# Hybrid decoder trunk on one core: where two weight loads and three small steps stand around the first and the last group's turn through memory in the MLP

## The chip, the core and the metric

The kernel runs on one core of a Trainium2 chip. The metric is the device time of one execution in microseconds; below it is given as the median of three runs. The profile is of one more execution, taken by the hardware profiler; all times inside it count from its first instruction. The engines are named as in the profile: PE (matrix multiplies; PEld its weight loads), ACT (scalar engine), DVE (vector engine), POOL (general engine) and SP, whose queue issues nearly all transfers.

## What is computed

Two layers of a mixer and an MLP over 256 tokens of width 1024, in fp32. The change lies in the MLP:

```python
def squared_relu_mlp(h, w_up, w_down):
    return jnp.square(jax.nn.relu(h @ w_up)) @ w_down
...
        h = rms_norm(x, mlp_norm[l])
        x = x + squared_relu_mlp(h, w_mlp_up[l], w_mlp_down[l])
```

`w_up` is 1024x4096, `w_down` 4096x1024. Fp32 products are made of three matmuls of rounded parts: with a high part and a low part (the rest) of each operand, high x high, high x low, low x high (`three`, L301 to L304).

## The kernel before

**Weights.** All weights lie in one array in the order of use, in blocks of 512 KB. SP's queue transfers a block to one of seven `raw` buffers (L218); ACT copies it to `whi` (rounded high part, L281), DVE subtracts to get `wlo` (L283), which frees the raw buffer. There are six `whi` and six `wlo`; a buffer of these is freed when PE has used it. So SP issues a transfer when DVE has split the block seven places earlier in the order.

**The MLP.** The 4096 hidden columns go in eight groups of 512. For each group four blocks `up` (i = 4g to 4g+3) are multiplied into two PSUM banks `pup`, one for each half of the tokens. `squared_relu(g)` (L1334) then reads the two banks with ReLU on ACT (L1338), squares the two halves on ACT (L1340), and DVE transposes 32x32 blocks of each (L332, `hblocks`). SP writes the result to memory (L346, `bounce`) and reads it back in four pieces (L350, `hturned`), which completes the transpose. `h_ready` (L1354) splits that into high part (ACT, L323 `sq`) and low part (DVE, L323 `sq`), the operands of the four blocks `down` of this group. Ten ups are done ahead; then PE's order, written out by hand in `mlp_order`, is for each group 0 to 4: down 4g, two ups, downs 4g+2 and 4g+3 together, down 4g+1, two ups. Groups 0, 1, 2, 3, 4 and 6 do those two downs together with seven products instead of eight (`seven`, L1383). For this `fetch_sums` (L243) makes sums of the two blocks on DVE (L240: `wsum` of down 4g+2 alone; `tsums`, the inner sums, of both) and `h_sums` sums of the operand (L1377 to L1379). Two of the seven products go to the PSUM banks of the group g+2 of `pup`, which was read just before; DVE copies (first group) or adds these to `carried` (L1411), and after that the banks serve the ups of group g+3. So after group 0's seven products, up 12 writes its first half into the bank of the second product and its second half into that of the first one, each after DVE's copy of it.

**What sets the order.** PE's order is fixed by hand in this stretch. On SP, ACT and DVE a scheduler with a model of time sets the order when the program is built; each engine then runs its list strictly in that order. `tc.issue_after(x)` (used through the table `behind` in `have`, L203) makes what a block of code issues on the engine of `x` stand behind `x` in that engine's list. It adds no wait. `behind[key]` so pins the transfer (if x is a transfer), the high part (if x is on ACT) or the sums and low part (if x is on DVE) of the block `key`. Before, for the first group two such pins stand at L1344: the raw transfer of down 4 behind the group's last `hturned`, and down 2's work on DVE behind the group's last transpose. `order` holds the blocks not fetched yet.

Of the kernel before, what the change touches and what calls it, by code (L numbers as in the profile page):

```python
# [10 lines left out]
AF = mybir.ActivationFunctionType  # L11
# [10 lines left out]
NF = DFF // P  # L22
# [134 lines left out]
def trunk(ctx: ExitStack, tc: tile.TileContext, gx, wts, consts, gfin, gn, xtok, out):  # L157


    nc = tc.nc  # L160
# [31 lines left out]
    order, loaded = list(where), {}  # L192
# [8 lines left out]
    behind = {}  # L201

    def have(n):  # L203

        while len(loaded) < n:
            first = order.pop(0)
            with ExitStack() as pinned:
                for ins in behind.get(first, ()):
                    pinned.enter_context(tc.issue_after(ins.ins))
                loaded[first] = fetch(first)  # L210
# [81 lines left out]
    def misc_tile(name="misc"):  # L292
        return ps.tile([P, 512], F32, name=name, tag="misc", bufs=4)

    def w2k(name):
        return sb.tile([P, 512], F32, name=name, tag="w2k", bufs=W2K)
# [31 lines left out]
    def blocks_tile(name):  # L328
        return sb.tile([P, 4 * S], F32, name=name + "blocks", tag="probT", bufs=2)

    def turn_row(blocks, t, row):
        return nc.vector.transpose(blocks.rearrange("p (b j t e) -> p t j b e", b=4, j=4, t=2)[:, t], row)  # L332

    def turned_blocks(rows, name, tag, bufs, last=None, then=()):

        blocks = blocks_tile(name)
        for t in range(NT):
            turn = turn_row(blocks, t, rows[t])
        for key in then:
            behind.setdefault(key, []).append(turn)  # L340
        return turned_by_hbm(blocks, name, tag, bufs, last)

    def turned_by_hbm(blocks, name, tag, bufs, last=None):

        bounce = dr.tile([P, 4 * S], F32, name="bounce", bufs=2)
        nc.sync.dma_start(bounce, blocks)  # L346
        turned = sb.tile([P, 4 * S], F32, name=name + "turned", tag=tag, bufs=bufs)
        for b in range(4):
            src = bounce.rearrange("(a p) (b r) -> b p a r", a=4, b=4)[b]
            dma = nc.sync.dma_start(turned[32 * b : 32 * b + 32, :].rearrange("p (a r) -> p a r", a=4), src)  # L350
        if last:
            behind.setdefault(last, []).append(dma)
        return turned
# [458 lines left out]
    def layer(l, xn, before):  # L812
# [4 lines left out]
        b0 = []  # L817
# [490 lines left out]
        us, h2, latest = {}, {}, []  # L1308

        def up(i):  # L1310

            g, j = divmod(i, 4)
            if j == 0:
                us[g] = [misc_tile("pup") for _ in range(NT)]
            wh, wl = load_w(l, "up", g, j)
            for kk in range(2):
                k = 2 * j + kk
                ah, al = xm.k(k)
                for t in range(NT):
                    sl = slice(P * t, P * t + P)  # L1320
                    three(us[g][t], ah[:, sl], al[:, sl], wh[:, kk, :], wl[:, kk, :], k == 0, k == KD - 1)
            if i == 1:
                xm.stats(accs[3])
            if j == 3:
                if g - 2 in SEVEN[l]:
                    have(2)
                    if g == 2:
                        with tc.issue_after(latest[1].ins):
                            sums[0] = h_sums(waiting.pop(0))
                elif g == NF // 4 - 1 and g - 1 in SEVEN[l]:  # L1330
                    have(4)
                squared_relu(g)

        def squared_relu(g):  # L1334

            rows = [w2k("relu") for _ in range(NT)]
            for t in range(NT):
                relu = nc.scalar.activation(rows[t], us[g][t], AF.Relu, scale=xm.col[t])  # L1338
            for t in range(NT):
                nc.scalar.activation(rows[t], rows[t], AF.Square)  # L1340
            if g:
                waiting[g] = turned_blocks(rows, "h", "t4", T4)
            else:
                waiting[g] = turned_blocks(rows, "h", "t4", T4, (l, "down", 4, 0), [(l, "down", 2, 0)])  # L1344
            if SEVEN[l][0] <= g - 2 < NF // 4 - 3:
                behind.setdefault(order[3 if g - 2 in SEVEN[l] else 4], []).append(relu)
            if 1 < g < NF // 4 - 1:
                h_ready(g - 1, relu)
            elif g != 1:
                h_ready(g)  # L1350

        waiting = {}

        def h_ready(g, after=None):  # L1354

            turned = waiting.pop(g)
            sq = sb.tile([P, 2, 4, S], F32R, name="sq", tag=("Q", "KK")[g % 2], bufs=1)
            with ExitStack() as pinned:
                if after:
                    pinned.enter_context(tc.issue_after(after.ins))  # L1360
                latest[:] = split_turned(turned, [sq[:, i] for i in range(2)])
            for j in range(4):
                h2[4 * g + j] = sq[:, 0, j, :], sq[:, 1, j, :]
            if g in SEVEN[l]:
                if not g or g - 1 in SEVEN[l]:
                    waiting[g] = turned
                else:
                    sums[g] = h_sums(turned)
# [89 lines left out]
        last = l == L - 1  # L1458
# [61 lines left out]
        if not last:  # L1520
            xn = Normed(G_ATT + KD * (l + 1), KD - 2)
            ys = {}


            have(ENDS[l])
            for j in range(ENDS[l], 4):
                behind[l + 1, "b0", j] = latest
            have(4)

            def copied(q):  # L1530
                ys[q] = w2k("ydn")
                copy = nc.vector.tensor_add(ys[q], accs[q], share[q])
                if q == 0:
                    tc.keep_in_program_order(copy)

            def turned(q):
                t, half = quarters[q]
                pt = misc_tile("pyd")
                for i in range(4):
                    nc.tensor.transpose(pt[:, P * i : P * i + P], ys[q][:, P * i : P * i + P], ident)  # L1540
                x_t = X[half][:, :, P * t : P * t + P]
                add = nc.vector.tensor_add(x_t, x_t, pt.rearrange("p (k s) -> p k s", k=4))
                if q == 0:
                    tc.keep_in_program_order(add)
                return xn.take_part(t, half)

            for q in range(4):
                ends[q]()
                copied(q)
                if q:  # L1550
                    turned(q - 1)

            def before(i):
                if i == 2:
                    behind[l + 1, "mq", 0, 0] = turned(3)
                if i == 7:
                    order_pe.close()

            return xn, before
# [44 lines left out]
    for l in range(L):  # L1604
        xn, before = layer(l, xn, before)
# [14 lines left out]
T4 = 8  # L1620
# [82 lines left out]
```

## Time and profile before

| what | value |
|---|---|
| median of three runs | 808.08 us (807.4 to 808.43) |
| profiled execution | 807.2 us, span of its instructions 805.4 us, granted clock 0.998 |
| PE busy | 797.0 us, 99% of the span |
| DVE, ACT busy | 675.8 us (84%), 483.1 us (60%) |
| transfers of raw weights | 264 of 512 KB, 4.9 us median from issue to landing |
| bounce, hturned of the MLP and the mixer | 16 of 512 KB, 3.6 us; 64 of 128 KB, 3.2 us |

A row of a timeline gives the start, the duration (from the first start to the last end where several equal instructions are merged), engine, line and operation; in brackets stands how long the engine had been idle before it and what ended that. Matmuls overlap: each is shown as 0.39 us, but one starts about 0.23 us after the other when nothing holds them up, so a hold-up is read from the starts. The first layer's MLP lies at about 221 to 397 us, the second's at about 620 to 800 us.

### The profile page before, as it was taken

How to read it: one execution, taken by the hardware profiler on the slowest of the kernel's cores; microseconds unless marked ns; L12 is line 12 of the kernel's file. 1: busy time of each engine (PE TensorE's matmuls, PEld its weight loads, DVE VectorE, ACT ScalarE, POOL GpSimd, SP SyncE). 2: the span in 40 equal slices, each digit the busy share in tenths (PEclk: the TensorE clock that was granted, in tenths of full speed). 3: DMA queues.
4: the chain of work that ended last, by engine and by line, in shares of the span. 5: the costliest groups of instructions: out<-in, count | busy, mean ns of one | idle time of the engine just before them, and what ended most of it. 6: DMA issues, size and time to landing. Idle time of an engine off the chain costs nothing.

```text
span 805.4 us, 11403 instructions
## 1 busy us (share of the span) xinstructions
PE 797.0 (99%) x3915; PEld 665.1 (83%) x3915; DVE 675.8 (84%) x1136; ACT 483.1 (60%) x747; POOL 73.2 (9%) x63
## 2 busy tenths in 40 slices
PE   9999999999999999999999999999999999999996
PEld 7888887888888888888788888888888878888885
DVE  6769997978888898887797987699698878899786
ACT  7775654653557666666486566655545666667562
POOL 0100810000030000000025220000000300000000
PEclk9999999999999999999999999999999999999999
DMA  9975889975678677778656579688665687788741
GB/s 335 338 244 179 281 241 297 282 235 173 222 225 244 228 255 248 252 269 259 209 163 228 157 232 326 213 261 273 217 223 192 186 272 260 241 280 319 261 169 54
DMA packets 68122, 192.11 MB, mean 239 GB/s; under 512 B 8288, under 2 KB 25056, under 8 KB 67808
## 3 DMA queue, kind: packets, MB, share of 16 engines
q1 hardware_dynamic: 67488, 190.71, 72.4%
q8 instruction: 31, 0.51, 0.3%
q10 hardware_dynamic: 576, 0.67, 0.2%
q14 instruction: 27, 0.22, 0.1%
HBM read 168.81 MB, written 18.87 MB: 233 GB/s over the span
## 4 chain that ended last, share of the span: by engine, by line
PE 89%; DMA 5%; DVE 3%; ACT 1%; SPq 1%; issue 1%; DVEq 0%; ACTq 0%
PE acc L302 16%; PE acc L304 16%; PE acc L303 16%; PE pup L302 6%; PE pup L304 6%; PE pup L303 6%; PE acc L1273 6%; PE acc L515 4%; PE acc L517 2%; DMA raw<-wts 2%; DMA hturned<-bounce 2%; DMA bounce<-hblocks 1%; PE ps_s L1039 1%; PE acc L881 1%; DMA qkoth<-qkraw 1%; DVE wlo L283 1%
## 5 line engine op out<-in xcount | busy, mean ns | idle before, releaser
L281 ACT ACTIVATE whi<-raw 128x1024 fp32r<-128x1024 f32 (+3 forms) x263 | 264.8, 1019 | 170.5 <-PE acc L304 98.1
L283 DVE TENSOR_TENSOR wlo<-raw,whi 128x1024 fp32r<-128x1024 f32 (+3 forms) x263 | 313.8, 1209 | 48.9 <-ACT whi L281 46.1
L302 PE MATMUL acc<-whi,xs 128*128 128x512 f32 (+1 forms) x304 | 119.4, 394 | 0.2
L303 PE MATMUL acc<-wlo,xs 128*128 128x512 f32 (+1 forms) x304 | 117.8, 388 | 0.0
L304 PE MATMUL acc<-whi,xs 128*128 128x512 f32 (+1 forms) x304 | 117.7, 388 | 0.0
L303 PE MATMUL pup<-wlo,xs 128*128 128x512 f32 x256 | 99.8, 390 | 0.0
L304 PE MATMUL pup<-whi,xs 128*128 128x512 f32 x256 | 99.6, 389 | 0.0
L302 PE MATMUL pup<-whi,xs 128*128 128x512 f32 x256 | 99.4, 389 | 0.0
L304 PE MATMUL acc<-whi,sq 128*128 128x512 f32 x184 | 72.0, 391 | 0.7 <-DVE sq L323 0.5
L302 PE MATMUL acc<-whi,sq 128*128 128x512 f32 x184 | 71.8, 390 | 0.0
L303 PE MATMUL acc<-wlo,sq 128*128 128x512 f32 x184 | 71.6, 389 | 0.0
L302 PEld LDWEIGHTS acc<-whi,xs 128*128 128x128 f32 x304 | 57.0, 188 | 13.6 <-issue 0.8
L304 PEld LDWEIGHTS acc<-whi,xs 128*128 128x128 f32 x304 | 57.1, 188 | 11.3
L303 PEld LDWEIGHTS acc<-wlo,xs 128*128 128x128 f32 x304 | 57.1, 188 | 10.7
L304 PEld LDWEIGHTS pup<-whi,xs 128*128 128x128 f32 x256 | 48.1, 188 | 9.9
L303 PEld LDWEIGHTS pup<-wlo,xs 128*128 128x128 f32 x256 | 48.1, 188 | 9.8
L302 PEld LDWEIGHTS pup<-whi,xs 128*128 128x128 f32 x256 | 47.9, 188 | 9.8
L606 ACT ACTIVATE prob<-prob,smx 128x128 f32<-128x128 f32 x64 | 28.3, 444 | 31.5 <-DVE smx L603 31.5
L391 POOL TENSOR_TENSOR sqsum<-sqsum,xsq 128x256 f32<-128x256 f32 x16 | 18.2, 1140 | 310.8 <-ACT xs L318 165.5
L304 PEld LDWEIGHTS acc<-whi,sq 128*128 128x128 f32 x184 | 34.5, 188 | 9.2 <-DVE sq L323 2.0
L323 DVE TENSOR_TENSOR sq<-hturned,sq 128x1024 fp32r<-128x1024 f32 x16 | 19.6, 1224 | 25.9 <-ACT sq L323 21.7
L515 PE MATMUL acc<-xs,whi 128*128 128x512 f32 x160 | 40.7, 395 | 0.4 <-ACT c L825 0.4
(275 smaller groups left out, 1398.7 us busy)
## 6 DMA issues: line engine op xcount, KB each, us to landing
raw<-wts SPq DMA_DIRECT2D x264, 512.0 KB, 4.9
bounce<-hblocks SPq DMA_DIRECT2D x16, 512.0 KB, 3.6
hturned<-bounce SPq DMA_DIRECT2D x64, 128.0 KB, 3.2
pbounce<-blocks SPq DMA_DIRECT2D x8, 768.0 KB, 4.0
probT<-pbounce SPq DMA_DIRECT2D x32, 192.0 KB, 5.9
qkoth<-qkraw SPq DMA_DIRECT2D x48, 64.0 KB, 4.8
raw<-wts SPq DMA_DIRECT2D x5, 464.0 KB, 6.1
dec<-consts SPq DMA_DIRECT2D x2, 1024.0 KB, 7.1
```

The costliest lines, as they stand in the source:

```text
L281: fetched.append(nc.scalar.activation(hi[:, cs], raw[:, cs], AF.Copy))
L283: nc.vector.tensor_sub(lo[:, cs], raw[:, cs], hi[:, cs].bitcast(F32))
L302: nc.tensor.matmul(o, ah, bh, start=start, stop=False, **more)
L303: nc.tensor.matmul(o, ah, bl, start=False, stop=False, **more)
L304: nc.tensor.matmul(o, al, bh, start=False, stop=stop, **more)
L323: return nc.scalar.activation(hi, src, AF.Copy), nc.vector.tensor_sub(lo, src, hi.bitcast(F32))
L391: (nc.gpsimd if n < self.on_pool else nc.vector).tensor_add(self.sum, self.sum, sq)
L515: nc.tensor.matmul(acc, wh[:, k, :], xn.both(k), start=k == 0, stop=False)
L517: nc.tensor.matmul(acc[:, 0:S], wl[:, k, :], xn.k(k)[0], start=False, stop=k == KD - 1)
L606: nc.scalar.activation(p[:, a:b], p[:, a:b], AF.Exp, bias=m[:, 2 + i : 3 + i], scale=d**-0.5, accum_out=m[:, 4 + i : 5 + i])
L881: nc.tensor.matmul(mq[n], wq[n][0], xn.both(k), start=k == 0, stop=False)
L1273: nc.tensor.matmul(o, a, b, start=half == 0 and i == 0, stop=4 * half + n == KD and i == len(jobs) - 1)
```

## The change

Four edits in the MLP:

- The last group's two squares on ACT go ahead of the high parts of the second and third block not fetched yet (`order[1:3]`), in both layers.
- First group: the raw transfer that is pinned behind the last `hturned` is that of up 13 (key `up, 3, 1`) instead of down 4's. Down 2's pin behind the last transpose is extended to down 3, whose block's fetch makes the inner sums (`tsums`).
- Last group of the first layer: the transfer of the next layer's block `b0, 2` is pinned behind its last `hturned`.
- The later pins of the next layer's blocks `b0` 2 and 3 are added to what is there instead of replacing it.

```diff
             for t in range(NT):
-                nc.scalar.activation(rows[t], rows[t], AF.Square)
+                squared = nc.scalar.activation(rows[t], rows[t], AF.Square)
+            if g == NF // 4 - 1:
+                for key in order[1:3]:
+                    behind.setdefault(key, []).append(squared)
             if g:
-                waiting[g] = turned_blocks(rows, "h", "t4", T4)
+                waiting[g] = turned_blocks(rows, "h", "t4", T4, None if last or g < NF // 4 - 1 else (l + 1, "b0", 2))
             else:
-                waiting[g] = turned_blocks(rows, "h", "t4", T4, (l, "down", 4, 0), [(l, "down", 2, 0)])
+                waiting[g] = turned_blocks(rows, "h", "t4", T4, (l, "up", 3, 1), [(l, "down", i, 0) for i in (2, 3)])
...
             for j in range(ENDS[l], 4):
-                behind[l + 1, "b0", j] = latest
+                behind.setdefault((l + 1, "b0", j), []).extend(latest)
```

PE's and POOL's lists stay as they were. SP, ACT and DVE change at the first and the last group of both layers.

SP's queue at the first two groups (the same rows in both layers), as a difference; the first `bounce` and the first four `hturned` are group 0's, the second ones group 1's:

```order
 L346 DMA bounce<-hblocks 128x1024
-L218 DMA raw<-wts 128x1024
+L350 DMA hturned<-bounce 32x4x256 x4
+L218 DMA raw<-wts 128x1024 x4
+L346 DMA bounce<-hblocks 128x1024
+L218 DMA raw<-wts 128x1024 x2
 L350 DMA hturned<-bounce 32x4x256 x4
 L218 DMA raw<-wts 128x1024 x3
```

The raw transfer between group 0's write and its reads (up 13's) now stands behind the reads. Between group 1's write and its reads now stand two raw transfers (down 6 and down 7) where one stood.

ACT in the first layer, first group, before. `relu_2543` and `relu_2544` are group 0's halves, `relu_2636` and `relu_2637` group 1's, `sq_2559` is group 0's high part; raw_2672 is down 0, 2692 and 2710 are up 10 and 11, 2728 and 2748 are down 2 and 3, `tsums` and `wsum` their sums:

```order
L233 ACTIVATE thi_2758<-tsums_2754 128x1024
L1340 ACTIVATE relu_2543<-relu_2543 128x512
L1340 ACTIVATE relu_2544<-relu_2544 128x512
L281 ACTIVATE whi_2674<-raw_2672 128x1024
L281 ACTIVATE whi_2694<-raw_2692 128x1024
L281 ACTIVATE whi_2712<-raw_2710 128x1024
L1338 ACTIVATE relu_2636<-pup_2562,ms_2502 128x512
L1338 ACTIVATE relu_2637<-pup_2563,ms_2502 128x512
L227 ACTIVATE sumhi_2732<-wsum_2730 128x512
L1340 ACTIVATE relu_2636<-relu_2636 128x512
L233 ACTIVATE whi_2750<-raw_2748 128x1024
L1340 ACTIVATE relu_2637<-relu_2637 128x512
L323 ACTIVATE sq_2559<-hturned_2554 128x1024
```

And now:

```order
L1340 ACTIVATE relu_2543<-relu_2543 128x512
L1340 ACTIVATE relu_2544<-relu_2544 128x512
L281 ACTIVATE whi_2674<-raw_2672 128x1024
L281 ACTIVATE whi_2694<-raw_2692 128x1024
L233 ACTIVATE thi_2758<-tsums_2754 128x1024
L281 ACTIVATE whi_2712<-raw_2710 128x1024
L323 ACTIVATE sq_2559<-hturned_2554 128x1024
L1338 ACTIVATE relu_2636<-pup_2562,ms_2502 128x512
L1338 ACTIVATE relu_2637<-pup_2563,ms_2502 128x512
L227 ACTIVATE sumhi_2732<-wsum_2730 128x512
L233 ACTIVATE whi_2750<-raw_2748 128x1024
L1340 ACTIVATE relu_2636<-relu_2636 128x512
```

The inner sums' high part (`thi`) stands behind group 0's squares and two high parts now, not ahead of the squares. Group 0's high part `sq_2559` has moved ahead of group 1's ReLU and squares. On DVE the same holds: the inner sums and their low part stand behind group 0's transposes, and group 1's transposes behind group 0's low part.

DVE a little later in the first layer, now (these rows stand so before too): `sq_2790` is group 1's low part, `hblocks_2780` group 2's transposes, raw_2872 is down 4, and the two copies empty the banks that up 12 writes next:

```order
L323 TENSOR_TENSOR sq_2790<-hturned_2647,sq_2790 128x1024
L332 STREAM_TRANSPOSE hblocks_2780<-relu_2774 128x4x4x32
L283 TENSOR_TENSOR wlo_2875<-raw_2872,whi_2874 128x1024
L1414 COPY carried_2802<-pup_2653 128x512
L332 STREAM_TRANSPOSE hblocks_2780<-relu_2775 128x4x4x32
L1414 COPY carried_2801<-pup_2652 128x512
```

Nothing has moved among these rows. At the last group, on ACT the two squares stand ahead of down 25's high part, where they stood behind it, and on DVE the transposes ahead of its low part; in the first layer SP's two raw transfers `b0, 2` and `b0, 3` stand behind the group's four reads, where one stood ahead of the write and one between write and reads.

## The prediction

> **What bounds the kernel now.** I read the engines' busy shares first, then PE's groups and timeline, then the chain of work that ended last.
>
> ```profile
> PE 797.0 (99%) x3915; PEld 665.1 (83%) x3915; DVE 675.8 (84%) x1136; ACT 483.1 (60%) x747; POOL 73.2 (9%) x63
> ```
>
> PE sets the time, and no matmul is added or removed. So only the places where PE is held up can give anything. In PE's timeline three starts are late, at the first group of each layer and the last group of the first one:
>
> ```profile
> 257.54 0.39 PE L303 MATMUL acc<-wlo,sq 128*128 128x512 f32 x1
> 258.05 0.50 PE L304 MATMUL acc<-whi,sq 128*128 128x512 f32 x1
> 258.38 0.39 PE L302 MATMUL acc<-whi,sq 128*128 128x512 f32 x1
> ...
> 389.89 0.39 PE L303 MATMUL acc<-wlo,sq 128*128 128x512 f32 x1
> 390.38 0.50 PE L304 MATMUL acc<-whi,sq 128*128 128x512 f32 x1
> 390.71 0.39 PE L302 MATMUL acc<-whi,sq 128*128 128x512 f32 x1
> ...
> 655.77 0.39 PE L303 MATMUL acc<-wlo,sq 128*128 128x512 f32 x1
> 656.68 0.50 PE L304 MATMUL acc<-whi,sq 128*128 128x512 f32 x1 [0.52 <-DVE sq L323]
> 657.02 0.40 PE L302 MATMUL acc<-whi,sq 128*128 128x512 f32 x1
> ```
>
> In each the third matmul of a down block waits for the low part of the squares. Against the usual step of 0.23 us the two steps lose 0.28 + 0.10 = 0.38 us (first layer, first group), 0.26 + 0.09 = 0.35 (first layer, last group) and 0.68 + 0.11 = 0.79 (second layer, first group): 1.52 us in all. The second layer's last group has none. That is all that the edits can win: 0.19% of 807.2 us.
>
> The chain shows what the first of these waits for:
>
> ```profile
> 242.06 0.70 DVE tsums L240
> ...
> 245.75 1.31 DVE hblocks L332 x2
> ...
> 247.08 2.61 DMA bounce<-hblocks
> ...
> 251.06 4.51 DMA hturned<-bounce
> ...
> 255.67 1.07 ACT sq L323
> ```
>
> DVE does the inner sums (which had waited for a raw transfer) ahead of the transposes; then comes the way through memory, where the last read takes 4.51 us; the high part of the squares, and the low part after it, come last.
>
> **First group: what is won.** On ACT
>
> ```profile
> 242.14 1.25 ACT L1338 ACTIVATE relu<-pup,ms 128x512 f32<-128x512 f32 x2
> ...
> 244.48 1.14 ACT L1340 ACTIVATE relu<-relu 128x512 f32<-128x512 f32 x2
> ```
>
> the squares now follow the ReLU directly, from 243.3 to 244.43. The transposes (1.31 us) follow the first square, 243.95 to 245.27, and the write starts at 245.3 instead of 247.08. The raw transfer ahead of it (up 12) moves too, since its buffer's low part stood behind the sums: from 244.71 to 243.5. How long writes and reads take depends on what is ahead of them:
>
> ```profile
> 244.71 0.33 SPq L218 DMA_DIRECT2D raw<-wts  x1
> ...
> 248.79 0.33 SPq L218 DMA_DIRECT2D raw<-wts  x1
> 249.74 1.75 SPq L350 DMA_DIRECT2D hturned<-bounce  x4
> ...
> 256.66 0.33 SPq L346 DMA_DIRECT2D bounce<-hblocks  x1
> ...
> 262.11 2.64 SPq L350 DMA_DIRECT2D hturned<-bounce  x4
> ...
> 273.02 0.33 SPq L346 DMA_DIRECT2D bounce<-hblocks  x1
> 276.63 1.75 SPq L350 DMA_DIRECT2D hturned<-bounce  x4
> ```
>
> A write with a raw transfer 2.4 us ahead took 2.61 us, the one at 273.02, with a raw 1.2 us ahead, 3.6 (its reads start at 276.63). With 1.8 us I take 3.0: landed at 248.3. Then four reads, the last issued 1.3 us after the first. Its time from issue to landing, in the views of the transfers of single stretches, is 3.1 us with nothing ahead (the one issued at 277.95), and 4.51 with the raw of 248.79 ahead:
>
> ```profile
> hturned<-bounce SPq DMA_DIRECT2D x1, 128.0 KB, 3.1
> ```
>
> That raw now stands behind, so 248.35 + 1.32 + 3.15 = 252.8. High part (1.07) 252.9 to 254.0, low part (1.2) to 255.3; PE wants it at 257.77. The stall goes, with 2.4 us to spare. The second layer runs the same list with the ReLU at 640.36, that is 398.2 us later. So **-0.38 and -0.79 us**.
>
> **Last group of the first layer.** The squares (and so the transposes) stop waiting for a high part of 1.06 us and a low part of 1.07:
>
> ```profile
> 374.81 1.06 ACT whi L281
> ...
> 375.89 1.07 DVE wlo L283
> ...
> 377.03 1.31 DVE hblocks L332 x2
> ```
>
> The write starts at 376.8 instead of 378.36, and the raw transfers beside it come after the reads. It is 1.5 us early against 0.26 wanted: **-0.35**. What is put behind (down 25's low part, now done by 378.1; `b0` transfers landing by some 386) is needed later: down 25 is PE's block ahead of down 28, so 2.7 us before 389.4, and `b0` comes after it. Covered; were it not, down 25 would be some 1.1 us later. In the second layer nothing was late, so nothing is won.
>
> **First group: what is late next.** ACT now does group 0's high part ahead of group 1's ReLU and squares. Before:
>
> ```profile
> 251.40 1.37 ACT L1338 ACTIVATE relu<-pup,ms 128x512 f32<-128x512 f32 x2 [0.98 <-PE pup L304]
> ...
> 254.65 0.62 ACT L1340 ACTIVATE relu<-relu 128x512 f32<-128x512 f32 x1
> ```
>
> ReLU to last square took 3.87 us. Now ACT sits idle until the reads of group 0 land at 252.8, and the ReLU starts only at 253.9, 2.5 us later; the last square ends at 257.65 (the same six operations, 3.76). On DVE down 3's low part (1.23) comes first, at 256.65 to 257.9, then the two transposes to 259.3. So group 1's write starts at 259.35 instead of 256.66. Its raw neighbours: up 15's transfer, freed by down 3's low part, at 257.9, that is 1.45 us ahead; the write takes some 3.35, not the 5.4 it took (256.66 to 262.11, with raws close ahead). It lands at 262.7, and the reads start at 262.75: only 0.65 late. But ahead of them in SP's queue now stand down 6's raw (at 260.7) and down 7's, which waits for down 1's low part (about 260.6 to 261.8) and goes at 261.85. From a raw issued ahead of the reads to the last landing the trace has 248.79 to 255.57, 6.8 us, and in the second layer
>
> ```profile
> 647.06 0.33 SPq L218 DMA_DIRECT2D raw<-wts  x1
> ...
> 649.59 4.62 DMA hturned<-bounce
> ```
>
> 7.1 (landed at 654.2); I take 6.95. A second raw 1.14 us before it adds what does not drain in between. Raws that queue land 1.3 us apart:
>
> ```profile
> raw<-wts SPq DMA_DIRECT2D x1, 512.0 KB, 5.0
> raw<-wts SPq DMA_DIRECT2D x1, 512.0 KB, 5.8
> ```
>
> (issued at 265.32 and 265.75, landed at 270.3 and 271.6), so 0.15. The last read lands at 261.85 + 6.95 + 0.15 = 268.95, the high part starts at 269.05. Who waits for that is seen here:
>
> ```profile
> 267.73 1.06 ACT L323 ACTIVATE sq<-hturned 128x1024 fp32r<-128x1024 f32 x1 [0.93 <-DMA hturned<-bounce]
> ...
> 268.82 1.23 DVE L323 TENSOR_TENSOR sq<-hturned,sq 128x1024 fp32r<-128x1024 f32 x1 [3.12 <-ACT sq L323]
> ...
> 272.91 0.65 DVE L1411 COPY carried<-pup 128x512 f32<-128x512 f32 x1
> ...
> 274.06 0.39 PE L302 MATMUL pup<-whi,xs 128*128 128x512 f32 x1
> ```
>
> PE itself needs group 1's operand only at 278.8. But on DVE the two copies of `carried` stand behind its low part, and up 12's second half waits for the second copy. From the start of the high part to the end of that copy it is 5.83 us (267.73 to 273.56), DVE without a pause; the spare before PE is 0.45. In the second layer it was 1.5:
>
> ```profile
> 670.53 0.66 DVE L1411 COPY carried<-pup 128x512 f32<-128x512 f32 x1
> ...
> 672.72 0.39 PE L302 MATMUL pup<-whi,xs 128*128 128x512 f32 x1
> ```
>
> With its stalls gone PE comes to this point at 274.06 - 0.38 = 273.68, and at 672.72 - 0.79 = 671.93, the same place in the list. The copy ends at 269.05 + 5.83 = 274.9. PE stands 1.25 us and restarts at a step 0.1 longer: **+1.35 us in each layer**. Bounds of this: with reads that take the 3.1 us of an empty queue the last lands at 267.2 and nothing is lost (0); with the 5.8 us of the slowest raw above it lands at 269.9, +2.3 us. I take the middle, as rows with a raw ahead are the nearest. The other steps that come later have room: down 1's low part ends at 261.8 and up 12's about 265, and PE comes to them after group 0's seven products, past 270.
>
> The Trainium skill ("DMA: Bandwidth & Descriptors", "Two DMAs through the same engine are not ordered") says that descriptors of one queue start in order, so reads issued behind a raw begin behind it. The trace agrees: 4.51 us behind the raw of 248.79, 3.1 with none ahead. The same page ("Bandwidth") gives about 358 GB/s for one core's side of the memory, by which 512 KB take 1.46 us (an estimate) where the landings here are 1.3 apart; by that each of the two new stalls would be about 0.15 longer, and the sum 0.3 worse, 809.6.
>
> **The sum.** -0.38 - 0.79 - 0.35 + 2 x 1.35 = +1.2 us. The profiled execution took 807.2 us (805.4 of span and 1.8 around it), so 808.4; the median of the runs shown is 0.9 higher, 808.08, and gives **809.3 us**. 0.2% is 1.6 us, about what a measurement of this kernel tells from no change; this is 0.15%.
>
> **Rivals.**
> - *The stall at up 12 does not come, or is small (faster).* If the second raw hardly delays the reads, the last lands by 267.7, the copy is in time, and all of 1.52 us is won: 806.55. For it: DVE had idled 3.12 us before group 1's low part. Against: the write cannot start before 259.2, and even a lone raw cost 1.4 us. Chance 0.15 for a stall under 0.8 us a layer; only its end goes beyond 0.2%.
> - *The reads fall far behind (slower).* If up 15's raw is issued right ahead of group 1's write, as before, when the write took 5.4 us, or both raws drain fully first, the stall is 2.3 us a layer: +3.1, 811.2. It passes 0.2% where group 1's high part starts later than about 269.25. Against: the earlier raws are done by then. Chance 0.32.
> - *The gain does not come*, because group 0's reads are late all the same: +2.7 without -1.17, +2.35, 810.4. ACT's list speaks against it; 0.03.
> - *My forecast*, a stall of 0.8 to 1.6 us a layer: 808.1 to 809.7. Chance 0.5.
>
> Range: 807.3 to 811.0. It leaves out the end of the first rival and of the second. Slower by over 0.2%: 0.34; within: 0.60; faster: 0.06, as the whole gain is just below 0.2%.
>
> **What would show it.** PE's third matmul of down 0 starts 0.23 us after the second in both layers, and down 28's in the first. ACT's group 1 ReLU starts near 253.9, its high part near 269. At up 12's second half PE's start is late, released by DVE's copy (L1414). If PE's starts there are even, the first rival holds; if the copies are in time but another row stalls, I am wrong about the place.

## The result, and the profile after

The change makes the kernel slower: a median of 817.1 us against 807.4 for the kernel before (five runs of each), a ratio of 1.0122 with a 95% interval of 1.0106 to 1.0139. Forecast were 809.3 us, a range of 807.3 to 811.0 and "within 0.2%".

The profiled execution took 821.2 us (span 819.4), the slowest of those timed; the others took 816.6 to 817.6. A second profile of the same kernel, shown further down, took 818.05. The engines' busy shares, where the kernel before had 99% for PE:

```profile
PE 801.4 (98%) x3915; PEld 668.2 (82%) x3915; DVE 675.0 (82%) x1136; ACT 482.0 (59%) x747; POOL 72.3 (9%) x63
```

The three late starts of the kernel before are gone. PE's timeline at down 0 of the first layer, down 28 of the first layer and down 0 of the second: each third matmul follows the second by 0.23 us.

```profile
258.69 0.39 PE L303 MATMUL acc<-wlo,sq 128*128 128x512 f32 x1
258.91 0.39 PE L304 MATMUL acc<-whi,sq 128*128 128x512 f32 x1
...
397.72 0.39 PE L303 MATMUL acc<-wlo,sq 128*128 128x512 f32 x1
397.94 0.39 PE L304 MATMUL acc<-whi,sq 128*128 128x512 f32 x1
...
663.28 0.39 PE L303 MATMUL acc<-wlo,sq 128*128 128x512 f32 x1
663.51 0.39 PE L304 MATMUL acc<-whi,sq 128*128 128x512 f32 x1
```

In their place PE stands twice, once in each layer, until a copy of `carried` is done. The waits grouped by who waited for whom (total, times, longest) say it in one row:

```profile
PE pup L302 <- DVE carried L1414: 9.9, 2, 5.3
```

PE's timeline at up 12, in the first layer and in the second:

```profile
273.87 0.39 PE L304 MATMUL acc<-whi,sq 128*128 128x512 f32 x1
279.55 0.79 PE L302 MATMUL pup<-whi,xs 128*128 128x512 f32 x1 [5.29 <-DVE carried L1414]
280.14 0.63 PE L303 MATMUL pup<-wlo,xs 128*128 128x512 f32 x1
280.57 0.63 PE L304 MATMUL pup<-whi,xs 128*128 128x512 f32 x1
...
678.47 0.39 PE L304 MATMUL acc<-whi,sq 128*128 128x512 f32 x1
683.49 0.79 PE L302 MATMUL pup<-whi,xs 128*128 128x512 f32 x1 [4.63 <-DVE carried L1414]
```

The block and the cause are the forecast ones; the size is not. Forecast was that up 12's second half waits for the second copy. PE stands already at its first half, for the first copy, as DVE's timeline shows; when it comes to the second half, at 281.00, the second copy is done:

```profile
278.82 0.68 DVE L1414 COPY carried<-pup 128x512 f32<-128x512 f32 x1
...
280.04 0.65 DVE L1414 COPY carried<-pup 128x512 f32<-128x512 f32 x1
```

The starts on PE are 5.68 and 5.01 us apart, that is 5.45 and 4.79 beyond a step of 0.23. And the matmuls behind are slow: 0.43 us apart. Stretches of the profile show why (the columns are the engines' busy time in the stretch, then the granted clock of PE, the share of the DMA engines and GB/s):

```profile
core 0: us, PE busy (x) PEld busy (x) DVE busy (x) ACT busy (x) POOL busy (x), PEclk, DMA share, GB/s
279.50:282.80 3.30, 3.25 (x8) 2.50 (x9) 3.30 (x6) 1.24 (x2) 0.00 (x0) 0.50 0.83 282
282.80:288.00 5.20, 5.20 (x24) 4.30 (x23) 5.20 (x8) 2.38 (x3) 0.00 (x0) 1.00 0.55 132
...
683.40:689.10 5.70, 5.62 (x13) 4.38 (x14) 5.70 (x10) 1.27 (x2) 0.00 (x0) 0.51 0.54 193
```

Behind the stand the granted clock is 0.50 for 3.3 us in the first layer and 0.51 in a stretch of 5.7 us in the second. By the count below this costs 1.7 and 2.7 us on top of the waits.

The chain of waits that ends at the late matmul (start, duration, what) runs twice through memory, for group 0 and then for group 1:

```profile
246.41 4.11 DMA bounce<-hblocks
...
251.89 3.07 DMA hturned<-bounce
...
255.07 1.06 ACT sq L323
256.13 1.16 ACT relu L1338 x2
...
261.45 4.43 DMA bounce<-hblocks
...
267.21 7.62 DMA hturned<-bounce
274.86 1.06 ACT sq L323
...
278.90 0.61 DVE carried L1414
```

Group 0's high part at 255.07, then group 1's ReLU, its write of 4.43 us, and a last read of 7.62 us. SP's queue shows what is ahead of that read (start of the issue, its duration, how many):

```profile
261.45 0.33 SPq L346 DMA_DIRECT2D bounce<-hblocks  x1
262.76 1.46 SPq L218 DMA_DIRECT2D raw<-wts  x2
265.90 1.75 SPq L350 DMA_DIRECT2D hturned<-bounce  x4
```

Two raws (transfers of a block of raw weights), issued while the write is under way. The second, of 263.90, took 8.3 us from issue to landing (512 KB):

```profile
raw<-wts SPq DMA_DIRECT2D x1, 512.0 KB, 8.3
```

It landed at 272.23, and the last read at 274.83, 2.6 us behind it.

### The profile page after: what moved, and what is told of

Same layout as the page of the kernel before. It is cut to its first block, busy times and chain, and to the rows that moved or that the text cites. A ratio compares the mean times of both kernels' runs of the same rounds, so it can differ in the third digit from the quotient of the medians.

```text
span 819.4 us, 11403 instructions
## 1 busy us (share of the span) xinstructions
PE 801.4 (98%) x3915; PEld 668.2 (82%) x3915; DVE 675.0 (82%) x1136; ACT 482.0 (59%) x747; POOL 72.3 (9%) x63
## 4 chain that ended last, share of the span: by engine, by line
PE 87%; DMA 6%; DVE 3%; ACT 2%; issue 1%; SPq 1%; DVEq 0%; ACTq 0%
PE acc L302 15%; PE acc L304 15%; PE acc L303 15%; PE pup L302 6%; PE pup L304 6%; PE pup L303 6%; PE acc L1273 5%; PE acc L515 4%; DMA hturned<-bounce 2%; PE acc L517 2%; DMA bounce<-hblocks 2%; PE ps_s L1039 1%; PE acc L881 1%; DMA qkoth<-qkraw 1%; DMA raw<-wts 1%
## 5 line engine op out<-in xcount | busy, mean ns | idle before, releaser
L302 PE MATMUL pup<-whi,xs 128*128 128x512 f32 x256 | 101.5, 398 | 9.9 <-DVE carried L1414 9.9
L304 PE MATMUL pup<-whi,xs 128*128 128x512 f32 x256 | 101.1, 395 | 0.0
L302 PEld LDWEIGHTS pup<-whi,xs 128*128 128x128 f32 x256 | 48.9, 192 | 21.1 <-DVE carried L1414 11.3
L304 PEld LDWEIGHTS pup<-whi,xs 128*128 128x128 f32 x256 | 49.0, 191 | 10.3
```

The lines of the kernel that those rows point to most:

```text
L302: nc.tensor.matmul(o, ah, bh, start=start, stop=False, **more)
L304: nc.tensor.matmul(o, al, bh, start=False, stop=stop, **more)
```

## The experiments

Beside each result stands a count of PE time, made in one way for all: the start of a PE instruction, less the start of the same instruction in the profile of the kernel before, taken just ahead of a place and behind it. The difference is what PE lost (+) or won (-) there, in us:

| kernel | down 0, 1st layer | up 12, 1st layer | down 28, 1st layer | down 0, 2nd layer | up 12, 2nd layer | sum |
|---|---|---|---|---|---|---|
| the change | -0.42 | +7.11 | -0.42 | -0.86 | +7.50 | +12.9 |
| the change, second profile | -0.43 | +5.51 | -0.43 | -0.87 | +6.56 | +10.3 |
| last group's edits only | +0.94 | 0 | -0.41 | +0.37 | 0 | +0.9 |
| squares first on ACT | -0.27 | +0.22 | -0.42 | -0.70 | +0.19 | -1.0 |
| no raw ahead | -0.43 | +1.67 | -0.42 | -0.87 | +1.84 | +1.8 |
| one raw ahead | -0.43 | +3.13 | -0.41 | -0.87 | +1.68 | +3.1 |
| copies first on DVE | -0.42 | 0 | -0.42 | -0.86 | 0 | -1.7 |
| reads' edit only | -0.26 | +0.14 | -0.42 | -0.70 | +0.43 | -0.8 |
| sums' edit only | -0.43 | +0.75 | -0.41 | -0.87 | +1.11 | +0.2 |
| copies first, no raw ahead | -0.43 | 0 | -0.41 | -0.86 | 0 | -1.7 |

Each row is one profiled execution; the times below are medians of several, and each ratio is against runs of the kernel before that were timed beside them (medians of 807.25 to 807.65 us). All diffs but that of the held kernels are against the changed kernel.

### The last group's edits alone

```diff
-                waiting[g] = turned_blocks(rows, "h", "t4", T4, (l, "up", 3, 1), [(l, "down", i, 0) for i in (2, 3)])
+                waiting[g] = turned_blocks(rows, "h", "t4", T4, (l, "down", 4, 0), [(l, "down", 2, 0)])
```

> The first group's two edits are undone (its reads are again ahead of down 4's raw only, and only down 2 stands behind its transposes); the last group's edits stay. Theory A (all of the loss comes from the first group): the late starts at down 0 are back in both layers, the one at down 28 of the first layer is gone, PE stands nowhere at up 12, and the time is the kernel before less 0.35 us: some 807.1, the same. Theory B (the last group's edits cost a part of the 9.7 us): over 808.5 us, with steps of PE above 0.23 us between 365 and 400 us.

Measured: 807.33 us, ratio 0.9993 (0.9983 to 1.0004). Theory A. Down 28's late start is gone (-0.41), the ones at down 0 are there again, in this execution even longer, and PE does not stand at up 12. All of the loss is the first group's. That 0.4 us are won is read from the trace; the time alone can't tell it from nothing.

### Group 1's ReLU and squares first on ACT

```diff
-            elif g != 1:
+            elif g == 1:
+                h_ready(0, squared)
+            elif g:
                 h_ready(g)
```

> The change as it is, but on ACT group 0's high part stands behind group 1's ReLU and squares, as before the change. Theory A (the loss begins with the 2.5 us by which that high part delays group 1's ReLU, and only then do two raws get ahead of group 1's reads): group 1's write starts near 257 us of the first layer instead of 261.45, one raw stands ahead of its reads, they land by about 268, PE does not stand at up 12; group 0's high part ends near 256.4 and its low part near 257.6, just before PE wants it at 257.77, so at most 0.3 us is lost at down 0. Sum: the kernel before less 1.2 to 1.5 us, 806.0 or so. Theory B (the reads are slow because the raws that the change moved behind group 0's reads now all run together with group 1's way through memory, whatever ACT does): group 1's reads still take over 6 us, PE stands over 2 us at up 12 in each layer, and the time is 811 us or more.

Measured: 806.56 us, ratio 0.9983 (0.9970 to 0.9996). Theory A, by more than 10 us against the change. ACT's timeline of the first layer: group 1's ReLU and squares, and only then group 0's high part:

```profile
250.66 1.37 ACT L1338 ACTIVATE relu<-pup,ms 128x512 f32<-128x512 f32 x2 [0.98 <-PE pup L304]
...
253.91 0.62 ACT L1340 ACTIVATE relu<-relu 128x512 f32<-128x512 f32 x1
254.43 1.05 ACT L323 ACTIVATE sq<-hturned 128x1024 fp32r<-128x1024 f32 x1
```

Group 1's write starts at 255.92, with the change at 261.45 (of these 5.5 us, 1.9 are that this execution runs so much ahead of the other from 140 us on). One raw stands between it and the reads, issued 3.8 us ahead of them; the last read lands at 267.14, and up 12 loses only 0.2 us a layer. Group 0's operand is just in time, which costs 0.16 us of each gain at down 0.

### No raw ahead of group 1's reads, and one

The first kernel holds the raws of down 6 and down 7 until group 1's reads are issued, the second only that of down 7 (`7` in place of `6`). ACT's order, and so the time of the write, stays that of the change.

```diff
-                waiting[g] = turned_blocks(rows, "h", "t4", T4, None if last or g < NF // 4 - 1 else (l + 1, "b0", 2))
+                hold = (l, "down", 6, 0) if g == 1 else None if last or g < NF // 4 - 1 else (l + 1, "b0", 2)
+                waiting[g] = turned_blocks(rows, "h", "t4", T4, hold)
```

> The change as it is, but the raw transfers of down 6 and down 7 wait until group 1's four reads are issued, so no raw stands ahead of these reads (the change: two). The write still starts at 261.45 us. Theory A (the two raws ahead in the queue are what made the reads long, 7.6 us from the issue of the last one): without them it takes 3 to 4.5 us as elsewhere with at most one raw ahead, the last lands near 270.5, the last copy ends near 276.3, and PE stands some 1.5 us in each layer instead of 5.7 and 5.0; 809 us, give or take 1. Theory B (the raws run side by side with the reads, in whichever order they are issued): the last read still takes over 6 us, PE stands over 3.5 us in each layer, 813 us or more.

Measured with none ahead: 809.44 us, ratio 1.0024 (1.0006 to 1.0042). Theory A, in time and in size. SP's queue and PE's timeline of this kernel in the first layer:

```profile
265.07 1.75 SPq L350 DMA_DIRECT2D hturned<-bounce  x4
266.92 1.82 SPq L218 DMA_DIRECT2D raw<-wts  x4
```

```profile
273.34 0.39 PE L304 MATMUL acc<-whi,sq 128*128 128x512 f32 x1
274.59 0.50 PE L302 MATMUL pup<-whi,xs 128*128 128x512 f32 x1 [0.86 <-DVE carried L1415]
```

The last read took 3.39 us (4.08 in the second layer), though four raws now follow right behind the reads. So it is the raws ahead that made the reads long, and the raws behind add little. The 1.7 to 1.8 us that PE still loses in each layer are the price of the late write alone.

> The change as it is, but of the two raws only down 6's stays ahead of group 1's reads; down 7's waits until they are issued. Theory A (each raw ahead costs the reads its own transfer): with none ahead the last read took 3.39 and 4.08 us and PE stood 1.0 and 1.2 us longer than a step; one raw of 512 KB adds 1.3 to 1.5, so 4.7 to 5.5 us, a stall of 2.3 to 2.7 us in each layer, and 811 to 812.5 us. Theory B (only the second raw, issued 2 us ahead of the reads, matters): as with none ahead, 809.5 us or so.

Measured with one ahead: 809.36 us, ratio 1.0019 (1.0006 to 1.0031). Theory B in the median: no worse than none, where theory A had priced this raw at 1.3 to 1.5 us a layer. (In its profiled execution up 12 lost 3.1 us in the first layer, where the write took 5.2 us, and 1.7 in the second.) Its queue:

```profile
261.97 0.33 SPq L218 DMA_DIRECT2D raw<-wts  x1
265.89 1.75 SPq L350 DMA_DIRECT2D hturned<-bounce  x4
```

The raw of 261.97 landed 1.17 us after the first read was issued (1.26 in the second layer), and the last read took 3.9 and 3.7 us. One raw has nearly drained when the reads come; the second, 1.1 us behind it, has not. That second raw makes the step from 809.4 to 817.1 us, the half clock behind the longer stand included.

### The copies first on DVE

The transfers stay as the change has them, two raws ahead of the reads. Group 1's high part goes behind group 2's squares on ACT, and its low part behind the two copies of `carried` on DVE.

```diff
+            last_square[:] = [squared]
...
-            if 1 < g < NF // 4 - 1:
+            if 2 < g < NF // 4 - 1:
                 h_ready(g - 1, relu)
-            elif g != 1:
+            elif g not in (1, 2):
                 h_ready(g)
...
+            if first:
+                with tc.issue_after(last_square[0].ins):
+                    h_ready(1, emptied[-1])
             if final:
```

> The change as it is, with the reads as late as they are, but group 1's high part stands behind group 2's squares on ACT, and its low part behind the two copies of carried on DVE. Theory A (PE stands at up 12 only because these copies stand behind that low part): PE does not stand at up 12, and group 1's operand itself, high part from 274.9 and low part done by about 277.5 in the first layer, is still in time for down 4, which PE reaches near 280 there; the time is the kernel before less the three stalls won, 806 us or so. Theory B (group 1's operand is needed itself, or its inner sums for the next seven products are): PE stands at down 4, or at the products of down 6, by over 1 us in each layer, and the time stays above 809 us.

Measured: 805.17 us, ratio 0.9967 (0.9954 to 0.9979), the fastest so far. Theory A. DVE's timeline and PE's at up 12:

```profile
269.06 1.25 DVE L1415 COPY carried<-pup 128x512 f32<-128x512 f32 x2
270.62 1.23 DVE L323 TENSOR_TENSOR sq<-hturned,sq 128x1024 fp32r<-128x1024 f32 x1 [0.31 <-ACT sq L323]
```

```profile
272.08 0.39 PE L304 MATMUL acc<-whi,sq 128*128 128x512 f32 x1
272.31 0.39 PE L302 MATMUL pup<-whi,xs 128*128 128x512 f32 x1
```

PE goes from the products into up 12 without a pause. So PE stood only because the copies were queued on DVE behind work that it did not need yet; group 1's operand was not too late for its own matmuls in this profile. The reads were not quick enough to explain it: the last one landed at 269.50, and with the 5.8 us from the landing to the end of the second copy that the change's order takes, PE would have waited some 2.4 us (an estimate; it reaches the second half at 272.99). In this execution the last reads behind the two raws landed 5.8 and 6.3 us after the first was issued, against 8.9 and 7.7 with the change; the second profile was made to see which of these is usual.

### The change once more

> The changed kernel once more, unaltered, for a second profile: in its first one the reads of group 1 behind two raws took 7.62 and 6.41 us (the last one, issue to landing), while behind the same two raws in the kernel with the copies first they took 4.47 and 5.01. Theory A (the order of the queue sets it, and PE's stall has the size of the first profile): again over 6 us in both layers, PE stands over 4.5 us in each at up 12. Theory B (how long reads behind two raws take varies from execution to execution): under 5.5 us in at least one layer, and PE stands under 4 us there; the chain from that landing to PE's restart stays at 4.7 to 4.8 us, and every microsecond of stall beyond some two is followed by a stretch of steps of 0.43 us.

Measured: 818.05 us. PE's timeline of the first layer, and two stretches of it:

```profile
273.41 0.39 PE L304 MATMUL acc<-whi,sq 128*128 128x512 f32 x1
276.88 0.50 PE L302 MATMUL pup<-whi,xs 128*128 128x512 f32 x1 [3.09 <-DVE carried L1414]
...
278.08 0.50 PE L302 MATMUL pup<-whi,xs 128*128 128x512 f32 x1 [0.23 <-DVE carried L1414]
```

```profile
276.80:278.70 1.90, 1.58 (x5) 1.02 (x6) 1.90 (x5) 1.26 (x2) 0.00 (x0) 0.95 0.74 192
278.70:281.70 3.00, 3.00 (x8) 2.31 (x7) 3.00 (x4) 0.00 (x0) 0.00 (x0) 0.50 0.56 228
```

Theory B, as the first layer has it: the last read took 5.30 us there and 5.93 in the second layer, and PE stood 3.25 and 4.89 us beyond a step. What theory A has right is that the loss is large each time, here 10.3 us. Where it varies, the landings show. From the landing of the second raw to that of the last read it took, in the ten cases with two raws ahead (both profiles of the change, both of the kernel with the copies first, and the sums' edit alone, two layers each), 2.4 to 2.9 us. What varies is the second raw itself, issued 1.5 to 3.1 us ahead of the reads: 5.3, 5.4, 5.9, 6.1, 6.1, 6.7, 6.9, 7.0, 7.0 and 8.3 us from issue to landing. In the kernel before, where one raw goes out 0.9 to 2.6 us ahead of the reads, when the write has about as long to go, it took 4.1 to 4.7 us; the one with 2.6 us to go, ahead of group 1's reads in the first layer, took 4.4. So the write alone does not make a raw as long as the second one is here; the first raw ahead of it adds to it.

### PE held without any transfer moved

Against the kernel before; the second kernel has `(7, 11)`. Nothing is computed otherwise, a copy is only repeated.

```diff
+            if first:
+                for _ in range((4, 16)[l]):
+                    nc.vector.tensor_copy(carried[1], moving[1])
             for i in (1, 0):
```

> The kernel before, where DVE repeats the first of the two copies of carried at the first seven products: 4 times more in the first layer, 16 times in the second, at 0.65 us each, less the spare of 0.45 and 1.5 us: PE is held some 2.2 us at up 12 in the first layer and 9 in the second, with no transfer moved. Theory A (a hold of PE is followed by steps of 0.43 us instead of 0.23 for some microseconds whatever caused it, so that the stall costs more than its length): slow steps behind the long hold, as behind the 5.0 and 5.7 us of the change (12 and 6 of them), perhaps none behind the short one. Theory B (the slow steps have to do with the transfers under way): none behind either.

> The same with 7 copies more in the first layer and 11 in the second: PE is held some 4.1 and 5.7 us. Theory A: slow steps behind both, 6 to 12 of them, 1.2 to 2.4 us in each layer on top of the hold. Theory B: none.

Their times, of one execution each, were 822.0 and 826.7 us. The holds came out, beyond a step, at 1.77 and 11.25 us in the first kernel, and 4.87 and 7.78 in the second. Stretches of the first kernel behind the short hold, and behind the long one:

```profile
276.40:280.00 3.60, 3.54 (x15) 2.93 (x16) 3.60 (x6) 0.09 (x1) 0.00 (x0) 1.00 0.56 156
...
685.40:689.50 4.10, 4.00 (x9) 3.14 (x10) 4.10 (x6) 0.63 (x1) 0.00 (x0) 0.50 0.43 122
```

Theory A. Half clock for 4.0 us behind the hold of 11.25, for 5.4 and 4.5 us behind those of 4.87 and 7.78, none behind that of 1.77; none either behind the stand of 2.49 us with one raw ahead:

```profile
275.90:279.00 3.10, 2.84 (x11) 2.06 (x12) 3.10 (x6) 1.22 (x2) 0.00 (x0) 1.00 0.84 288
```

Counted as in the table, the three long holds cost 2.0, 2.7 and 2.3 us more than their lengths, and the four long stands of the two profiles of the change 1.7 to 2.7. So a long stand costs PE 1.7 to 2.7 us more than its length, whatever caused it, and the extra does not grow with the length.

### Each of the first group's two edits alone

The first kernel keeps the edit of the reads, the second that of the sums; the last group's edits stay in both.

```diff
+                waiting[g] = turned_blocks(rows, "h", "t4", T4, (l, "up", 3, 1), [(l, "down", 2, 0)])
...
+                waiting[g] = turned_blocks(rows, "h", "t4", T4, (l, "down", 4, 0), [(l, "down", i, 0) for i in (2, 3)])
```

> Of the first group's two edits only the first: the raws from down 4 on wait for group 0's reads (up to up 13's raw), but only down 2 stands behind the transposes, as before the change; the last group's edits stay. ACT's order is then the one before the change (group 1's ReLU and squares ahead of group 0's high part), and one raw stands ahead of group 1's reads. Theory A (the stall at down 0 came from the raw ahead of group 0's reads): the write starts at 247.1 as before, the reads at 249.8 land by 254.2 instead of 255.57, the high part starts when the squares end (255.3), 0.37 us earlier than before, about as much as the first layer's late start; PE does not stand at up 12; the kernel before less 0.35, 0.3 and 0.6 or so: 806.4. Theory B (the inner sums ahead of the transposes are what made group 0 late): the late starts at down 0 stay, 807.2.

Measured: 806.47 us, ratio 0.9986 (0.9974 to 0.9998). Theory A. Reads without a raw ahead are enough to undo most of the late starts at down 0; the write starts as late as before (247.51 us, in an execution that is 0.5 us late as a whole).

> Of the first group's two edits only the second: down 3 stands behind the transposes too, but up 13's raw still stands ahead of group 0's reads. On ACT group 0's high part then falls between group 1's two squares, and two raws stand ahead of group 1's reads. Theory A (the loss comes from the two raws ahead of group 1's reads, the second issued while the write is under way): the last read lands some 2.5 us behind the second raw, after 270 us of the first layer, and the copy of carried that stands behind the low part is late: PE stands 1 to 4 us in each layer, 809 to 815 us. Theory B (it comes from the 2.5 us by which ACT is held ahead of group 1's ReLU): the ReLU goes as before, so PE does not stand at up 12, and 806.5 us.

Measured: 809.3 us, ratio 1.0022 (1.0006 to 1.0038); its profiled execution was a quick one, 806.5. Theory A by the median; in the quick execution PE stood only 0.6 and 1.0 us beyond a step. ACT's timeline and SP's queue of the first layer:

```profile
250.73 1.37 ACT L1338 ACTIVATE relu<-pup,ms 128x512 f32<-128x512 f32 x2 [0.98 <-PE pup L304]
...
253.89 1.06 ACT L323 ACTIVATE sq<-hturned 128x1024 fp32r<-128x1024 f32 x1 [0.75 <-DMA hturned<-bounce]
...
255.81 0.62 ACT L1340 ACTIVATE relu<-relu 128x512 f32<-128x512 f32 x1
```

```profile
258.33 0.33 SPq L346 DMA_DIRECT2D bounce<-hblocks  x1
259.64 1.67 SPq L218 DMA_DIRECT2D raw<-wts  x2
263.19 1.75 SPq L350 DMA_DIRECT2D hturned<-bounce  x4
```

The ReLU goes in time, the second square waits for the high part, and again two raws stand ahead of the reads (the second took 7.0 us) and PE stands. So the edit of the sums brings the loss, through the order that the planner then gives ACT and the queue. Alone it costs some 2 us; with the edit of the reads, group 0's reads come sooner, ACT takes the high part ahead of the ReLU too, and it is 9.7. The edit of the reads without that of the sums loses nothing: of its row of -0.8 us, 0.4 are the reads' edit and 0.4 the last group's.

### The versions that beat both

> The kernel with the copies of carried ahead of group 1's low part once more, with more rounds. Theory A: its gain is that of the three late starts, in its trace 0.40, 0.41 and 0.84 us, and nothing else: a ratio of 0.998, 805.9 to 806.1 us for a kernel before at 807.6. Theory B (it wins more, as its first time of 805.17 us says): 0.9967 again.

> The same, and no raw ahead of group 1's reads (down 6 and down 7 wait for them). Theory A (no late start is left for it to win): the same time as with the copies first alone, within 0.1%. Theory B (earlier reads still win something, as the spare for group 1's operand is small in some executions): some 0.5 us less; a loss would say that down 6 or down 7 now comes too late for their products.

The second adds to the copies first the hold of down 6 and down 7 shown above. Measured: 805.26 us, ratio 0.9980 (0.9971 to 0.9989), and 805.04 us, ratio 0.9974 (0.9966 to 0.9983). Theory A for both: the trace counts -1.7 us for each, 0.21% of 807, and both intervals hold it; the 0.9967 of the first comparison is 0.1% below. The two don't differ by what this measurement tells. Either beats the kernel before and the change.

## Why the prediction was wrong

**What was right.** The three late starts go, for 0.42, 0.42 and 0.86 us where 0.38, 0.35 and 0.79 were put (down 0 and down 28 of the first layer, down 0 of the second). The last group's edits cost nothing. The new stall is at the block where it was put, though half a block earlier, in both layers, and by the mechanism named: ACT does group 0's high part first, group 1's write comes late, two raws get ahead of its reads, and the copies of `carried` stand behind its low part. The experiments undo each link in turn, and the stall shrinks or goes each time.

**What failed** is the term of this stall: +1.35 us per layer, bound 2.3. It measured 7.1 and 7.5 us, in the second profile 5.5 and 6.6. The second profile's first layer shows the steps beside the predicted ones. This execution runs 0.68 us later than that of the kernel before from 140 us on, and PE comes to the second copy 0.6 us later than predicted. So some 0.65 us of each later point of time in the table is this shift and no error; the durations are free of it. PE wants the second copy four steps of 0.23 us behind the last matmul at 273.41; what PE lost behind its wait is the 5.5 us of the count above less the wait:

| step, first layer | predicted | measured |
|---|---|---|
| group 0's write starts, and takes | 245.3, 3.0 | 245.95, 3.93 |
| group 0's last read lands | 252.8 | 254.38 |
| group 1's write starts, and takes | 259.35, 3.35 | 260.87, 4.64 |
| down 7's raw is issued | 261.85 | 263.31 |
| from there to the last read's landing | 7.1 | 8.84 |
| last read lands | 268.95 | 272.15 |
| second copy ends | 274.9 | 278.02 |
| PE wants it | 273.68 | 274.3 |
| PE waits | 1.25 | 3.8 |
| behind the wait | 0.1 | 1.7 |

Three things were mis-sized, one behind the other on one chain. (1) The write with a raw 1.75 us ahead took 3.93 us, not 3.0: I had drawn a line between two rows, 2.61 and 3.6 us, and the raw ahead of it took 4.4 us itself. Group 0's high part, and with it group 1's ReLU and write, came later by it: without the shift, down 7's raw was issued 0.8 us late. (2) "A second raw 1.14 us before it adds what does not drain in between", 0.15 us: the stretch from that raw to the last read's landing came out 1.7 us longer here, and 3.8 in the first profile (263.90 to 274.83). The 6.95 us in it were read from raws that go out when the write has 1 us to go and no raw is ahead; here the second raw goes out with 2.2 us of the write and a whole raw ahead of it, since group 1's write took 4.64 us and not 3.35. The Trainium skill ("DMA: Bandwidth & Descriptors", "Two DMAs through the same engine are not ordered") says that descriptors within one queue of one engine start in order. The landings 2.4 to 2.9 us behind the second raw agree with reads that begin behind what the queue still holds. The 0.8 us of (1) and the 1.7 of (2) are PE's wait of 3.8 us in place of 1.25. (3) The restart after the wait was priced at 0.1 us, from stalls of 0.3 to 0.7 us. Behind a wait of 3.25 us and more it is half clock.

On that third point the trace came first: 0.50 behind every stand of 3.25 us or more, 1.00 behind 1.77 and 2.49. The Trainium skill ("TensorE: Matmul & The Clock Gate", "What's actually happening") says that PE falls to half clock after an idle window of some 3.4 us and needs about as long busy to come back. The half clock of 3.3 to 5.5 us behind the restarts agrees roughly; the stand of 3.25 us was a little shorter than the window, and there the clock fell only some 1.6 us after the restart (the stretch of 276.80 to 278.70 has a mean of 0.95). By the runs here, a stall of over 3 us as the bad end would have had to carry 1.7 to 2.7 us more in each layer. I held 2.3 us to be the end, and so put nothing for it.

The way from the high part to the copies was judged rightly: 5.83 us from the start of the high part to the end of the second copy were put, 5.84 measured in the second profile.

**The rivals.** The one with the reads far behind had the sign, the place and the cause, and its price was the same bound of 2.3 us. The errors of (1) and (2) both lengthen a wait whose spare was already used up, so they went into the time whole, and (3) came on top, from a length of stand that neither end of the range reached.

**What stays open** is why the second raw takes 5.3 us in one execution and 8.3 in another, behind the same queue. From the start of group 1's write to the last read's landing the DMA engines were 0.97 busy in the first layer of both the slowest case (the change's first profile) and the quickest (the first profile with the copies first), but moved 267 GB/s in the one and 311 in the other: the engines were as busy and each transfer took longer. What slowed them no run here shows. Nor do they show at what length of stand the half clock sets in: 2.49 us did not bring it, 3.25 us did.

## What to carry to other kernels

A chain that goes twice through one DMA queue must be sized by what is left in the queue at the moment of issue, not by the nearest case with as many transfers ahead; a write still under way counts too. When an operand comes in late and is not needed yet, put its operations behind the ones that release a buffer which PE waits for: that order took the late reads off PE's path and kept the gain. When an edit removes a stall, read the planner's new order beyond that place too: here ACT, freed of one late step, was given the next late one, group 0's high part, ahead of group 1's ReLU, which was due first.

## What was not expected of the hardware

A stand of PE has a price with a step in it. Behind 2.49 us or less the next matmuls ran 0.23 us apart; behind 3.25, 4.79, 4.87, 4.89, 5.45, 7.78 and 11.25 us they ran 0.43 us apart for some 3.3 to 5.5 us, at a granted clock of 0.50. And a raw of 512 KB, which landed in about 3.5 us when it was issued with no other transfer under way (at 271.80 in the kernel before, at 260.04 with the change), took 3.9 to 5.3 us as the only one behind a write that was under way, and 5.3 to 8.3 us as the second.
